# Twelve background modulation tasks move from the SSD groups to the attention heads, and a convolution's first tap from VectorE to ScalarE

## The chip, the cores and the metric

The kernel runs on one core of one Trainium2 chip. The metric is the device time of one execution in microseconds (us), the median of several runs. A core has five engines with an instruction queue each: TensorE (PE, matrix products; PEld is its weight load), VectorE (DVE), ScalarE (ACT), GpSimd (POOL) and SyncE (SP), which here issues the transfers. Each engine takes its instructions in order and waits at an instruction until its inputs are there and its output's buffer is free.

## The reference

A decoder trunk of two layers on 1024 tokens of width 1024, in float32. Layer 0 runs a Mamba-2 mixer beside a differential attention and then an MLP; layer 1 runs retention beside sliding-window attention and then an MLP. Before each sublayer the input is normalized, scaled and shifted, and after it the output is normalized and gated; scale, shift and gate are rows of a matrix product of the conditioning vector with a modulation matrix. What the change touches:

```
xbc = silu(causal_depthwise_conv(xbc, conv_w, conv_b))      # 4 taps per channel, 2048 channels
xs, Bs, Cs = split_cols(xbc, ...)                           # SSD in 4 groups of 4 heads
y = ssd_chunked(xh, dt, A, Bs, Cs)                          # 8 chunks of 128 tokens
...
q, k, v = ...                                               # differential attention: 8 heads
p = softmax(q1 k1 + bias) - lam * softmax(q2 k2 + bias)     # two maps a head, causal
out = rms_norm(p @ v)
...
shift, scale, gate = split(silu(c) @ mod_w + mod_b, 3)      # for each of 4 sublayers
```

## The kernel before, in words

Every product with a weight is made of three matmuls on float32 values that are split into a high and a low part. A weight block is loaded with one transfer of 0.5 or 1 MB into one of **two** buffers named `raw` (`raw_cols`, L163, and `load_group`, L185), its high part is cast by ACT (`wh`, L156) and its low part subtracted on POOL or DVE (`wl`, L158). Products whose results lie with features on the partitions are L454 to L456 (512 columns), those with tokens on the partitions L808 to L810 (256 columns).

The even mixer runs four SSD groups (g = 0 to 3), then the eight attention heads, then the output projection (`MixerOut`). In an SSD group the gate `zs` is made by products L808 to L810 and DVE (L843). Four convolutions (`conv`) follow, each of an ACT copy of the product into `xc` (L1006), a first tap `ch` on DVE (L1079), three more taps on DVE (L1082), a tanh on ACT (L1085) and a product on DVE (L1086); PE transposes the result (L1119). In a chunk, `xdt` on DVE (L1125) is an input of PE's L1132. In an attention head the weights of q and k (512 KB each) and, in head 0 and every second head after it, those of v for the next pair of heads (1 MB) are loaded first (`load_fm`, `v_half`). Eight query blocks follow from the widest (1024 keys) to the narrowest (128): PE makes the scores of both maps (L867, L868), DVE adds the bias and takes the maximum (L1225), ACT the exponential (L1228), DVE the reciprocals (L1233, L1234) and the difference of the maps (L1238), PE transposes it (L1245, `pat`), the copy L1247 brings it back to SBUF, PE multiplies with v (L1251, `pav`), ACT sums the squares (L1255), POOL takes the power (L135), and DVE scales the block (L1258), which SP writes out (L1260). `pat`, `pav` and `pgate` (below) share two PSUM tiles (`pt`), and the scores two larger ones.

The scheduler of the framework (it orders by a timeline of its own) sets the order of the instructions on each engine; instructions with work for later may be pulled ahead of those written before them, and PE's products for the next head stand among those of the current one, where their weights are there. Here they are called fillers.

The **background tasks** stand in a queue `bgq`: during the even mixer 12 tasks, four each for the gate of the current sublayer and the shift and the scale of the next. A task loads 1 MB of the modulation matrix into a `raw` buffer (L292) and adds it up, weighted, with two DVE operations into the only tile `macc` (L297 for the first, L299 for the others). The fourth task of each four ends with `fin`: it splits the sum into `parts` (L198 on ACT, L199 on DVE), and `parts` takes a `raw` buffer too. For the gate, PE multiplies `parts` with ones (L316, `pgate`), DVE adds the bias (L317), and SP loads `gpost` (L319), which takes the tile `macc` until DVE has used it (L320). A call of `bg()` takes `bg_n[0]` tasks from the queue; it stands in `raw_cols` and in `load_group`, so each load of weights is followed by that many tasks. `bg_n[0]` is 1 in the groups g = 2 and 3 (five calls a group), and the scheduler pulled the first of them ahead into g = 1. Ten tasks are done there, the last two in `MixerOut`.

Of the kernel before, what the change touches and what calls it, by code (L numbers as in the profile page):

```python
# [12 lines left out]
AF = mybir.ActivationFunctionType  # L13
ALU = mybir.AluOpType
# [5 lines left out]
D = 1024  # L20
# [8 lines left out]
def trunk(ctx: ExitStack, tc: tile.TileContext, x, c, rel_bias, norm_gains, mod_w, mod_b, mlp_w1, mlp_w2,  # L29
          e_w_in, e_conv_w, e_conv_b, e_dt_bias, e_A_log, e_D, e_ssd_norm, e_lambda, e_diff_norm, e_w_out,  # L30
          o_w_in, o_sinks, o_w_out, k_mat, k_onehot, k_mask, k_rope, k_ret, out, subs=(0, 1, 2, 3)):
    nc = tc.nc
# [27 lines left out]
    def turn(i):  # L60

        turns[i] = 1 - turns.get(i, 1)
        return turns[i]

    def slot(i, shape, dtype=F32, name="slot"):

        return slots.tile(shape, dtype, tag=f"s{i}", name=name)
# [73 lines left out]
    bg_n, in_mlp = [0], [False]  # L141
# [698 lines left out]
    def silu2(th, dst, src):  # L840

        nc.scalar.activation(th, src, AF.Tanh, scale=0.5)
        nc.vector.scalar_tensor_tensor(out=dst, in0=th, scalar=1.0, in1=src, op0=ALU.add, op1=ALU.mult)  # L843
# [153 lines left out]
    def even_mixer(prev, late):  # L997
# [11 lines left out]
        def silu_tmp():  # L1009
            return slot(4 + turn(4), [P, 256], F32, "th")  # L1010
# [10 lines left out]
        def z_dt(ts):  # L1021
            for t in ts:
                ps = tok_unit(z_blks, t, 272, early[t // 2][:, t % 2] if t < 4 else None)
                nc.vector.tensor_tensor(out=dt[:, t], in0=ps[:, 256:272], in1=hv[:, 0], op=ALU.add)
                silu2(silu_tmp(), zs0[t // 4][:, t % 4], ps[:, 0:256])
# [5 lines left out]
        with ExitStack() as st:  # L1031
            mp = st.enter_context(pool("ssd"))
            cw = sm[:, 6, 0:80].rearrange("p (i k) -> p i k", i=5)
            nc.vector.tensor_scalar(out=cw[:, 0:4], in0=cols[:, 1, 0:64].rearrange("p (i k) -> p i k", i=4),
                                    scalar1=0.5, scalar2=None, op0=ALU.mult)
# [9 lines left out]
            def time_steps():  # L1045
                flat = dt.rearrange("p c h -> p (c h)")
                softplus(flat)
                nc.vector.scalar_tensor_tensor(out=dA, in0=dt, scalar=-1.0,
                                               in1=hv[:, 1].unsqueeze(1).broadcast_to([P, 8, 16]),
                                               op0=ALU.mult, op1=ALU.mult)  # L1050
                nc.vector.tensor_copy(out=dAh, in_=dA)
                nc.vector.tensor_tensor(out=dAl, in0=dA, in1=dAh.bitcast(F32), op=ALU.subtract)
                for lhs, dst in ((upper, ecs), (kmat[:, 2], d2e), (ones, cdec)):
                    ps = pt.tile([P, 512], F32, tag="t", name="pcs")
                    mm(ps[:, 0:P], lhsT=lhs, rhs=dA.rearrange("p c h -> p (c h)"), start=True, stop=True)
                    nc.scalar.activation(dst.rearrange("p c h -> p (c h)"), ps[:, 0:P], AF.Exp)

            for g in range(4):
                lo_on[0] = nc.gpsimd if g else nc.vector
                zs = zs0  # L1060
                if g == 0:
                    z_dt(range(4, NT))
                    time_steps()
                    bias_rows()
                else:
                    bg_n[0] = 1 if g >= 2 else 0
                    zs = [slot(g % 2 * 6 + i, [P, 4, 256], F32, "zs") for i in range(2)]
                    proj_tok(w, g * 256, 256, lambda t, ps: silu2(silu_tmp(), zs[t // 4][:, t % 4], ps))

# [2 lines left out]
                def conv(key, ft, c0, given=None):  # L1072

                    xc, rest = given or conv_in(c0)
                    if rest:
                        rest()
                    ft_c = ft
                    h = slot(12 + turn(12), [P, D], F32, "ch")
                    nc.vector.tensor_scalar(out=h, in0=xc[:, 0:D], scalar1=cw[:, 0, ft_c:ft_c + 1],  # L1079
                                            scalar2=cw[:, 4, ft_c:ft_c + 1], op0=ALU.mult, op1=ALU.add)  # L1080
                    for i in range(1, 4):
                        nc.vector.scalar_tensor_tensor(out=h, in0=xc[:, i:i + D], scalar=cw[:, i, ft_c:ft_c + 1],  # L1082
                                                       in1=h, op0=ALU.mult, op1=ALU.add)
                    o = slot({"b": 8, "c": 9, "x0": 10, "x1": 11}[key], [P, D], F32, f"fm{key}")
                    nc.scalar.activation(o, h, AF.Tanh)  # L1085
                    nc.vector.scalar_tensor_tensor(out=o, in0=o, scalar=1.0, in1=h, op0=ALU.add, op1=ALU.mult)  # L1086
                    fm[key] = o
# [8 lines left out]
                for ci in range(NT):  # L1096
# [37 lines left out]
                    if ci:  # L1134
# [7 lines left out]
                                                   op0=ALU.mult, op1=ALU.mult)  # L1142
# [24 lines left out]
        with ExitStack() as st:  # L1167
# [6 lines left out]
            for i in range(2):  # L1174
# [5 lines left out]
                                           op0=ALU.add, op1=ALU.subtract)  # L1180
# [15 lines left out]
                             ts=range(8) if h == 0 else range(4) if h % 2 else range(4, 8))  # L1196

            lo_on[0] = nc.gpsimd
            for h in range(8):

                places = ((12, 13, 2, 3, 4, 16), (19, 18, 14, 15, 5, 17))[h % 2]
# [11 lines left out]
                for qb in reversed(range(NT)):  # L1213
# [3 lines left out]
                    for m in range(2):  # L1217
                        ps = both[:, m] if nk <= 512 else pw("psc").rearrange("p a b -> p (a b)")
                        for n0 in range(0, nk, 512):
# [16 lines left out]
                                            op0=ALU.mult, op1=ALU.mult)  # L1236
# [13 lines left out]
                    for kb in range(qb + 1):  # L1250
# [8 lines left out]
                                            op0=ALU.mult, op1=ALU.mult)  # L1259
                    nc.sync.dma_start(out=yd[2 + h // 4][:, qb, (h % 4) * P:(h % 4 + 1) * P], in_=ys)  # L1260

            lo_on[0] = nc.vector
            mo = MixerOut(0, e_w_out[0], yd, (0, 1, 2, 3), lambda g: rs if g < 2 else None,
                          lambda g, f: cols[:, 0, 120 + g * 4 + f:121 + g * 4 + f] if g < 2 else dn,
                          None)
# [328 lines left out]
```

## Time and profile before

| what | value |
|---|---|
| median of 3 runs | 3029.69 us (3027.28 to 3030.26) |
| the profiled execution's own time | 3030.93 us |
| its span from the first to the last instruction | 3029.1 us |
| instructions | 40060 |
| PE busy | 2929.4 us, 97% of the span |
| DVE, ACT, POOL busy | 66%, 43%, 16% of the span |
| mean granted TensorE clock | 0.986 |

The span is what the profiler saw; 1.8 us of the profiled execution lie around it. An engine is busy when an instruction of it is under way; instructions of one engine overlap by some hundredths of a us at their ends, so that a sum of durations is above the busy time. A granted clock of 1.00 is 2.4 GHz, 0.50 is 1.2 GHz.

### The profile page before, as it was taken

Reading aid. Unit: us, or ns where it says so; the run is one execution under the profiler, and the core shown is the slowest. Engines: PE = TensorE matmul, PEld = TensorE weight load, DVE = VectorE, ACT = ScalarE, POOL = GpSimd, SP = SyncE. Lnnn points to the kernel's source line nnn. Section 1 sums busy time; section 2 is a strip of 40 time slices with the busy share of each in tenths; the row PEclk is TensorE's granted clock in tenths of the full one; section 3 lists DMA queues with packets and bytes.
Section 4 is the critical chain, followed back from the end, with each engine's and each line's share of the span. In section 5 each row is a group of like instructions: output and inputs, shape, how many; then the busy total and the mean of one; then the engine's idle time right before and its main releaser. Section 6 shows DMA issues by size and latency. Waiting matters only on the chain.

```text
span 3029.1 us, 40060 instructions
## 1 busy us (share of the span) xinstructions
PE 2929.4 (97%) x15250; PEld 2471.4 (82%) x15250; DVE 1991.2 (66%) x3222; ACT 1309.4 (43%) x2348; POOL 474.2 (16%) x430
## 2 busy tenths in 40 slices
PE   8999999999999989999999989999999899999998
PEld 5888879888877867888888878989988678888887
DVE  5787885565586579876646845565454876666476
ACT  5232334555553264454433545432222644454333
POOL 0243443323210030000000232011101200000021
PEclk9999999999999999999999999999999999999999
DMA  6221311212142236646736542153242454476464
GB/s 215 75 89 57 120 53 46 66 41 61 46 150 71 89 127 217 221 163 235 290 125 226 191 134 63 33 168 101 84 153 77 140 188 162 153 260 231 151 223 166
DMA packets 268707, 413.59 MB, mean 137 GB/s; under 512 B 15337, under 2 KB 151138, under 8 KB 267618
## 3 DMA queue, kind: packets, MB, share of 16 engines
q1 hardware_dynamic: 268128, 410.92, 40.3%
q8 instruction: 120, 1.97, 0.3%
q14 instruction: 73, 0.60, 0.1%
q10 hardware_dynamic: 386, 0.11, 0.0%
HBM read 319.23 MB, written 91.75 MB: 136 GB/s over the span
## 4 chain that ended last, share of the span: by engine, by line
PE 81%; DVE 10%; DMA 4%; ACT 2%; issue 2%; POOL 1%; SPq 0%; POOLq 0%; DVEq 0%; ACTq 0%
PE pw L740 5%; PE pw L741 5%; PE pw L742 5%; PE pw L557 4%; PE pg L454 4%; PE pg L456 4%; PE pg L455 4%; PE pw L558 4%; PE pw L559 4%; PE pg L808 4%; PE pg L809 3%; PE pg L810 3%; PE pg L466 3%; PE pg L468 3%; PE pg L467 3%; PE pg L740 2%
## 5 line engine op out<-in xcount | busy, mean ns | idle before, releaser
L156 ACT CAST wh<-raw 128x1024 fp32r<-128x1024 f32 (+1 forms) x218 | 227.5, 1047 | 294.7 <-PE pw L558 97.7
L808 PE MATMUL pg<-wh,hh 128*128 128x256 f32 (+1 forms) x992 | 292.4, 295 | 18.5 <-DVE zs L843 10.6
L454 PE MATMUL pg<-hh,wh 128*128 128x512 f32 x736 | 292.8, 398 | 1.4 <-DVE ks L1340 0.8
L456 PE MATMUL pg<-hh,wl 128*128 128x512 f32 x736 | 291.9, 397 | 0.3 <-DVE ms L133 0.3
L455 PE MATMUL pg<-hl,wh 128*128 128x512 f32 x736 | 291.9, 397 | 0.0
L810 PE MATMUL pg<-wh,hl 128*128 128x256 f32 (+1 forms) x992 | 287.5, 290 | 0.6 <-DVE hl L439 0.6
L809 PE MATMUL pg<-wl,hh 128*128 128x256 f32 (+1 forms) x992 | 287.4, 290 | 0.0
L158 DVE TENSOR_TENSOR wl<-raw,wh 128x1024 fp32r<-128x1024 f32 (+1 forms) x162 | 199.3, 1232 | 130.3 <-ACT wh L156 127.4
L510 ACT CAST u<-uraw 128x1024 fp32r<-128x1024 f32 x112 | 117.1, 1049 | 299.8 <-PE pw L741 178.2
L511 DVE TENSOR_TENSOR u<-uraw,u 128x1024 fp32r<-128x1024 f32 x112 | 141.1, 1261 | 154.5 <-ACT u L510 153.7
L741 PE MATMUL pw<-wl,u 128*128 128x512 f32 x608 | 240.3, 395 | 0.0
L740 PE MATMUL pw<-wh,u 128*128 128x512 f32 x608 | 240.1, 396 | 0.0
L742 PE MATMUL pw<-wh,u 128*128 128x512 f32 x608 | 239.4, 394 | 0.0
L135 POOL TENSOR_TENSOR rs<-ms,expo 128x1 f32<-128x1 f32 x160 | 107.3, 671 | 682.2 <-DVE ms L133 664.2
L808 PEld LDWEIGHTS pg<-wh,hh 128*128 128x128 f32 x992 | 193.8, 195 | 21.9 <-DVE zs L843 10.3
L810 PEld LDWEIGHTS pg<-wh,hl 128*128 128x128 f32 x992 | 193.1, 195 | 2.5 <-DVE hl L439 1.3
L809 PEld LDWEIGHTS pg<-wl,hh 128*128 128x128 f32 x992 | 193.7, 195 | 1.8 <-issue 0.5
L466 PE MATMUL pg<-wh,u 128*128 128x512 f32 x448 | 181.9, 406 | 3.6 <-DVE u L940 3.1
L468 PE MATMUL pg<-wh,u 128*128 128x512 f32 x448 | 178.2, 398 | 0.0
L467 PE MATMUL pg<-wl,u 128*128 128x512 f32 x448 | 177.5, 396 | 0.0
L158 POOL TENSOR_TENSOR wl<-raw,wh 128x1024 fp32r<-128x1024 f32 x58 | 144.2, 2490 | 138.2 <-ACT wh L156 119.3
L454 PEld LDWEIGHTS pg<-hh,wh 128*128 128x128 f32 x736 | 139.1, 189 | 29.5 <-PE pg L456 1.2
(456 smaller groups left out, 7242.2 us busy)
## 6 DMA issues: line engine op xcount, KB each, us to landing
x<-in_mlp_w_dram SPq DMA_DIRECT2D x128, 512.0 KB, 6.6
uraw<-ud SPq DMA_DIRECT2D x56, 1024.0 KB, 5.5
raw<-in_mod_w_dram SPq DMA_DIRECT2D x24, 1024.0 KB, 5.0
ud<-sums SPq DMA_DIRECT2D x48, 512.0 KB, 4.2
raw<-in_mlp_w_dram SPq DMA_DIRECT2D x18, 1024.0 KB, 5.4
raw<-in_e_w_in_dram SPq DMA_DIRECT2D x32, 512.0 KB, 3.9
ud<-c SPq DMA_DIRECT2D x64, 256.0 KB, 3.1
mraw<-in_mod_w_dram SPq DMA_DIRECT2D x32, 512.0 KB, 4.9
```

The source lines that it names most:

```text
L158: lo_on[0].tensor_tensor(out=wl, in0=src, in1=wh.bitcast(F32), op=ALU.subtract)
L454: mm(ps, lhsT=wh[:, k], rhs=hh[:, k], start=(k == 0), stop=False)
L455: mm(ps, lhsT=wh[:, k], rhs=hl[:, k], start=False, stop=False)
L456: mm(ps, lhsT=wl[:, k], rhs=hh[:, k], start=False, stop=(k == 7))
L466: mm(ps, lhsT=uh[:, tl], rhs=wh[:, f % 2], start=(f == 0), stop=False)
L468: mm(ps, lhsT=ul[:, tl], rhs=wh[:, f % 2], start=False, stop=(f == 3))
L740: mm(ps[t], lhsT=uh[:, k, ts], rhs=wh[:, k], start=b, stop=False, **on)
L741: mm(ps[t], lhsT=uh[:, k, ts], rhs=wl[:, k], start=False, stop=False, **on)
L742: mm(ps[t], lhsT=ul[:, k, ts], rhs=wh[:, k], start=False, stop=e, **on)
L808: mm(ps[:, 0:n], lhsT=hh[:, k, tl], rhs=wh[:, i], start=(k == 0), stop=False)
L809: mm(ps[:, 0:n], lhsT=hh[:, k, tl], rhs=wl[:, i], start=False, stop=False)
L810: mm(ps[:, 0:n], lhsT=hl[:, k, tl], rhs=wh[:, i], start=False, stop=(k == 7))
```

## The change

`bg_n[0] = 1` is taken from the groups g = 2 and 3 and set for the loop over the eight attention heads; it is set to 0 again ahead of `MixerOut`. So the 12 tasks are called from the first 12 loads of the heads. Beside that, the first tap of each of the 16 convolutions becomes an activation with the function Identity on ACT; it reads the same tile and writes the same tile.

```diff
                 else:
-                    bg_n[0] = 1 if g >= 2 else 0
                     zs = [slot(g % 2 * 6 + i, [P, 4, 256], F32, "zs") for i in range(2)]
...
                     h = slot(12 + turn(12), [P, D], F32, "ch")
-                    nc.vector.tensor_scalar(out=h, in0=xc[:, 0:D], scalar1=cw[:, 0, ft_c:ft_c + 1],
-                                            scalar2=cw[:, 4, ft_c:ft_c + 1], op0=ALU.mult, op1=ALU.add)
+                    nc.scalar.activation(h, xc[:, 0:D], AF.Identity, scale=cw[:, 0, ft_c:ft_c + 1],
+                                         bias=cw[:, 4, ft_c:ft_c + 1])
...
             lo_on[0] = nc.gpsimd
+            bg_n[0] = 1
             for h in range(8):
...
             lo_on[0] = nc.vector
+            bg_n[0] = 0
             mo = MixerOut(0, e_w_out[0], yd, (0, 1, 2, 3), lambda g: rs if g < 2 else None,
```

Line numbers between 1080 and 1198 of the kernel before are lower by one in the changed kernel, those between 1199 and 1262 are the same.

The first place is DVE at the end of the convolutions of group g = 1, where the gate `zs` of g = 2 is made. Before:

```order
L299 SCALAR_TENSOR_TENSOR macc<-raw,cact,macc 128x1024
L1086 SCALAR_TENSOR_TENSOR fmx_1862<-fmx_1862,ch 128x1024
L299 SCALAR_TENSOR_TENSOR macc<-raw,cact,macc 128x1024
L1105 TENSOR_TENSOR rh<-kmat,dAh 128x512
L1079 TENSOR_SCALAR ch<-xc,sm 128x1024
L1114 TENSOR_TENSOR cbm<-pssd,kmat 128x128
L1082 SCALAR_TENSOR_TENSOR ch<-xc,sm,ch 128x1024
L1114 TENSOR_TENSOR cbm<-pssd,kmat 128x128
L1115 TENSOR_TENSOR dec<-dec,cbm 128x512
L1082 SCALAR_TENSOR_TENSOR ch<-xc,sm,ch 128x1024
L1115 TENSOR_TENSOR dec<-dec,cbm 128x512
L843 SCALAR_TENSOR_TENSOR zs<-th,pg 128x256
```

After:

```order
L1085 SCALAR_TENSOR_TENSOR fmc<-fmc,ch 128x1024
L1081 SCALAR_TENSOR_TENSOR ch<-xc,sm,ch 128x1024 x3
L1104 TENSOR_TENSOR rh<-kmat,dAh 128x512
L1085 SCALAR_TENSOR_TENSOR fmx_1862<-fmx_1862,ch 128x1024
L1104 TENSOR_TENSOR rh<-kmat,dAh 128x512
L1113 TENSOR_TENSOR cbm<-pssd,kmat 128x128
L1114 TENSOR_TENSOR dec<-dec,cbm 128x512
L1113 TENSOR_TENSOR cbm<-pssd,kmat 128x128
L1114 TENSOR_TENSOR dec<-dec,cbm 128x512
L1081 SCALAR_TENSOR_TENSOR ch<-xc,sm,ch 128x1024
L843 SCALAR_TENSOR_TENSOR zs<-th,pg 128x256
```

The two L299 and the L1079 ahead of the first `zs` are gone from DVE here; the other rows are the same work in nearly the same order.

The second place is SP at the entry of the attention heads. The first 256-column load of `raw` (1 MB) shown is of v's weights for heads 2 and 3, the 128-column ones are of q and k of a later head, `ye_399` is the output of the SSD and `ye_400` that of head 0. Before:

```order
L1172 DMA lam<-in_e_lambda_dram 128x256
L1144 DMA ye_399<-y 128x256 x2
L994 DMA bt_4026<-vd 128x256
L163 DMA raw<-in_e_w_in_dram 128x8x256
L994 DMA bt_4027<-vd 128x256
L163 DMA raw<-in_e_w_in_dram 128x8x128 x2
L1260 DMA ye_400<-ys 128x128 x3
L163 DMA raw<-in_e_w_in_dram 128x8x256
```

After (the task at the top is the fifth, the first of the shift):

```order
L163 DMA raw<-in_e_w_in_dram 128x8x128
L994 DMA bt_3955<-vd 128x256
L292 DMA raw<-in_mod_w_dram 128x2x1024
L1260 DMA ye_400<-ys 128x128 x5
L994 DMA bt_3954<-vd 128x256
L1260 DMA ye_400<-ys 128x128 x3
L163 DMA raw<-in_e_w_in_dram 128x8x256
L292 DMA raw<-in_mod_w_dram 128x2x1024
```

The load of v's weights for heads 2 and 3 stood ahead of all outputs of head 0 and stands now behind all eight. There it waits for PE, which must have read the gate's `parts` (made in g = 3's convolutions, where the scheduler puts the four tasks of the gate); the other `raw` buffer holds the fifth task's block, whose DVE operation needs `macc` and so stands behind `gpost`. The gate's `fin` belongs to the fourth task, which is called from head 1's first load, so that `pgate` takes its PSUM tile after those of head 0.

The third place is PE in head 0. Before, a part of its block loop, with the product for v of heads 2 and 3 (L808 to L810) between `pat` and `pav`:

```order
L808 MATMUL pg<-wh,hh_114 128x256
L809 MATMUL pg<-wl,hh_114 128x256
L810 MATMUL pg<-wh,hl_115 128x256
L454 MATMUL pg<-hh_114,wh 128x512
L455 MATMUL pg<-hl_115,wh 128x512
L456 MATMUL pg<-hh_114,wl 128x512
L454 MATMUL pg<-hh_114,wh 128x512
L455 MATMUL pg<-hl_115,wh 128x512
L1251 MATMUL pav<-v,aT 128x128 x4
L867 MATMUL psc_4681<-ks,qh 128x256
L868 MATMUL psc_4681<-ks,ql 128x256
L456 MATMUL pg<-hh_114,wl 128x512
```

After, the last rows of head 0's loop:

```order
L1245 MATMUL pat<-kmat,p 128x128 x3
L1251 MATMUL pav<-v,aT 128x128 x3
L867 MATMUL psc_4658<-ks,qh 128x128
L868 MATMUL psc_4658<-ks,ql 128x128
L1245 MATMUL pat<-kmat,p 128x128 x2
L1251 MATMUL pav<-v,aT 128x128 x2
L1245 MATMUL pat<-kmat,p 128x128
L1251 MATMUL pav<-v,aT 128x128
L316 MATMUL pgate<-parts,onesr 128x512 x4
L808 MATMUL pg<-wh,hh_114 128x256 x2
L809 MATMUL pg<-wl,hh_114 128x256
L810 MATMUL pg<-wh,hl_115 128x256
```

The products L808 to L810 for heads 2 and 3 (96 of them) and the next 48 products of 512 columns for q and k stood in head 0's loop; now they stand behind it and behind `pgate`, and in the last seven blocks of the loop scores, transposes and outputs follow each other with nothing else between them.

## Rows read from the trace of the kernel before

**Rows 1.** The page: span, and TensorE's busy time, share and instructions.
```profile
span 3029.1 us, 40060 instructions
...
PE 2929.4 (97%) x15250; PEld 2471.4 (82%) x15250; DVE 1991.2 (66%) x3222; ACT 1309.4 (43%) x2348; POOL 474.2 (16%) x430
```

**Rows 2.** Windows: us, busy us of PE, PEld, DVE, ACT, POOL (instructions), clock, DMA.
```profile
180.00:275.00 95.00, 88.70 (x516) 78.16 (x515) 81.03 (x111) 29.17 (x66) 39.05 (x34) 0.96 0.24 77
275.00:370.00 95.00, 89.32 (x523) 79.37 (x522) 79.34 (x107) 29.42 (x62) 39.49 (x32) 0.96 0.31 95
489.90:551.20 61.30, 61.30 (x380) 54.92 (x379) 36.35 (x97) 35.94 (x82) 17.50 (x14) 1.00 0.18 52
```

**Rows 3.** What PE waited for, 80 to 500 us: total, times, longest.
```profile
PE pg L808 <- DVE zs L843: 9.5, 2, 5.5
PE pxt L1119 <- DVE fmx L1086: 4.0, 2, 2.6
PE py L1132 <- DVE xdt L1125: 3.9, 2, 2.5
```

**Rows 4.** Windows in which TensorE ran at half clock.
```profile
228.10:234.90 6.80, 5.17 (x24) 5.17 (x25) 6.64 (x8) 1.06 (x1) 0.10 (x1) 0.50 0.25 104
323.70:330.50 6.80, 3.66 (x17) 3.66 (x18) 6.80 (x8) 1.05 (x1) 2.37 (x1) 0.50 0.40 136
972.20:979.00 6.80, 5.05 (x12) 3.99 (x13) 6.12 (x6) 0.48 (x1) 0.00 (x0) 0.50 0.64 195
```

**Rows 5.** DVE in time order in group g=2: start, duration, instruction.
```profile
319.01 1.27 DVE L299 SCALAR_TENSOR_TENSOR macc<-raw,cact,macc 128x1024 f32<-128x1024 f32 x1
320.20 2.85 DVE L1079 TENSOR_SCALAR ch<-xc,sm 128x1024 f32<-128x1024 f32 x1
...
326.38 0.41 DVE L843 SCALAR_TENSOR_TENSOR zs<-th,pg 128x256 f32<-128x256 f32 x1
```

**Rows 6.** Operations on the convolution's tile, durations min/median/max in ns.
```profile
L1079 DVE TENSOR_SCALAR ch<-xc,sm x16: 800/1138/2887, 88.3 to 421.8; 128x1024 f32<-128x1024 f32 x16
L1085 ACT ACTIVATE fmx<-ch x8: 1057/1060/1064, 119.0 to 428.0; 128x1024 f32<-128x1024 f32 x8
```

**Rows 7.** Operations on the accumulator of the background tasks.
```profile
L299 DVE SCALAR_TENSOR_TENSOR macc<-raw,cact,macc x42: 1259/1280/3420, 172.1 to 2139.6; 128x1024 f32<-128x1024 f32 x42
```

**Rows 8.** What PE waited for in the output projection, 960 to 990 us.
```profile
PE pg L466 <- DVE u L940: 3.1, 1, 3.1
```

**Rows 9.** DVE in time order in attention head 0.
```profile
489.99 1.23 DVE L1225 CUSTOM_DVE_ANT_0 psc<-psc,bt 128x1024 f32<-128x1024 f32 x1 [2.10 <-PE psc L868]
...
497.09 1.10 DVE L1225 CUSTOM_DVE_ANT_0 psc<-psc,bt 128x896 f32<-128x896 f32 x1 [0.83 <-PE psc L868]
...
550.82 0.41 DVE L1258 TENSOR_SCALAR ys<-pav,rs,rc 128x128 f32<-128x128 f32 x1
```

**Rows 10.** PE in time order: first and last of 15 filler matmuls.
```profile
543.77 0.40 PE L454 MATMUL pg<-hh,wh 128*128 128x512 f32 x1
...
546.98 0.39 PE L456 MATMUL pg<-hh,wl 128*128 128x512 f32 x1
```

**Rows 11.** Groups by shape, 488 to 560 us: count, busy us, mean ns.
```profile
L158 POOL TENSOR_TENSOR wl<-raw,wh 128x1024 fp32r<-128x1024 f32 x6 | 14.3, 2394 | 11.4 <-ACT wh L156 10.6 <-PE psc L868 0.8
...
L156 ACT CAST wh<-raw 128x1024 fp32r<-128x1024 f32 x5 | 5.3, 1052 | 5.6 <-PE pg L455 5.2 <-issue 0.4
...
L873 POOL MEMSET ql<- 64x1024 f32 x2 | 1.9, 949 | 0.1
...
L1228 ACT ACTIVATE p<-psc,mx 128x128 f32<-128x128 f32 x2 | 0.7, 364 | 0.3 <-DVE rc L1233 0.3
...
L1225 DVE CUSTOM_DVE_ANT_0 psc<-psc,bt 128x128 f32<-128x128 f32 x2 | 0.6, 300 | 2.6 <-PE psc L868 2.6
...
L1238 DVE SCALAR_TENSOR_TENSOR p<-p,rc 128x128 f32<-128x128 f32 x1 | 0.4, 354 | 0.0
```

**Rows 12.** DMA issues, 478 to 484 us: KB each, us to landing.
```profile
raw<-in_e_w_in_dram SPq DMA_DIRECT2D x1, 1024.0 KB, 5.2
```

## The prediction

> **What bounds the kernel now.** I read the page first: TensorE is busy 97% of the span [rows 1], so time is won only where PE stands still or runs at half clock, and lost where either is new. The windows by stage come next. In the SSD groups g=1 and g=2, PE lacks 6.3 and 5.7 us of 95, while DVE is busy 81 and 79 us and ACT only 29 in each; in attention head 0 PE is busy all 61.3 us, with DVE and ACT at 36 [rows 2]. So the moved work leaves a stage where DVE is nearly full and enters one where it has room, and the question is what order it makes there. The waits say what PE lacks in the SSD: `zs` twice (5.5 and, the rest of 9.5, 4.0 us), `fmx` (2.6 and 1.4), `xdt` [rows 3]. Each of the two `zs` waits is accompanied by 6.8 us at half clock, and so is one stretch in the output projection [rows 4]. DVE in time order shows the cause in g=2: an L299 of a background task, then an L1079 that takes 2.85 us, and only at 326.38 the `zs` for which PE waits [rows 5]. L1079 takes 0.80 us at its fastest, 1.14 in the median [rows 6].
>
> **What it gives back.** The order shows both parts at work at that place: the L299 and the L1079 ahead of `zs` are gone.
> - g=1: the `zs` wait of 4.0, the `fmx` wait of 1.4, and half of the 5.17 us for which PE worked at half clock, 2.6 [rows 3, 4]: 8.0 us.
> - g=2: 5.5, and half of 3.66, 1.8: 7.3 us [rows 3, 4].
> - g=3: nothing. Four first taps leave DVE, but the scheduler puts the gate's four tasks (eight operations of 1.28 us [rows 7]) and the split there, about as much as left. Its waits, 2.6 for `fmx` and 3.9 for `xdt` [rows 3], could go or double; I take 0, between +4 and -4.
> - Output projection: PE waited 3.1 us for `u`, which was queued on DVE behind an L299, and worked 5.05 us at half clock after it [rows 8, 4]: at most 5.6. The last two tasks leave, but a weight load of 1 MB still has to come there; I take 4.5.
>
> Sum 19.8 us, between 12 and 26. The taps' 16 activations cost nothing on ACT by this: beside them stands a tanh of the same shape at 1.06 us [rows 6], 4.2 us a group, and ACT is free for two thirds of a group.
>
> **What it takes.** The fact that decides is in the order of SP and PE. Both `raw` buffers are held through head 0: one by `parts` until `pgate`, one by the fifth task. So the load of v's weights for heads 2 and 3 cannot start before `pgate`, and `pgate` stands behind head 0's last output. The 96 products of 256 columns for that v, and 48 of 512 columns behind them, thereby leave the loop that they filled, and about as many more of 512 columns that came from head 2's early loads.
>
> *The bare loop.* Before, from the first maximum at 489.99 to the last scaled block at 550.82 [rows 9] PE was busy without a gap. Fillers come at (546.98-543.77)/14 = 0.229 us [rows 10], half of that for 256 columns. 96 of each kind are 22 and 11 us, and some 3 us are head 1's first scores, so head 0's own work on PE is about 26 us. How fast can the blocks run without fillers? From the first block's first maximum to the second block's it is 7.1 us [rows 9]: scores, two maxima, an exponential, the difference, one behind the other. The 128-wide block has two maxima of 0.30, an exponential of 0.36, a difference of 0.35 [rows 11], and about 1 us of reciprocals and hand-overs as in the wide one: 2.3 us. Eight blocks falling from 7.1 to 2.3 are 38 us, and the last block's transpose, copy, product and scaling add some 3. Laid out row by row in the new order with these durations I come to 42 us from the first maximum to `pgate`. PE idles 42-26 = 16 us. The lower bound is DVE's own work: 36.35 us [rows 2] less some 6 us for other heads, so 30, idle 4. The upper one is a loop in which PE is at half clock throughout: 52 us, loss 26.
>
> *POOL.* Two clears of 0.95 us [rows 11] stand there between the powers that the scaled blocks wait for, each behind a wait for PE: 2 us.
>
> *The clock in the loop.* In the rows of half clock, PE had stood for 4 to 5.5 us just before or within [rows 3, 4]. A loop with 16 us of gaps should be granted half clock for part of it; idle PE absorbs most of that. I take 3 us, between 0 and 10.
>
> *The wait behind it.* After `pgate`: 5.2 us of transfer [rows 12], a cast of 1.05 on ACT, a subtraction of 2.39 on POOL [rows 11]: PE stands 8.6 us. Nothing is ready in the order to cover it, since the 48 products whose weights are there stand behind. By the two `zs` waits, such a gap is followed by 6.8 us at half clock: 3.4 us more.
>
> *Heads 1 to 3.* Tasks 5 to 12 bring 16 operations of 1.28 us to a DVE that is free for 40% of the time [rows 2]; each next block is loaded when its predecessor has been added. Tasks 5 to 8 run under the 96+48 products (22 us) behind `pgate`. I take 1 us, up to 5 if the last of them delays head 1's first maximum.
>
> Sum 16+2+3+8.6+3.4+1 = 34 us. Net +14: the profiled execution's 3030.9 would become 3045; that execution lies 1.2 us above the median of the runs, so the median goes from 3029.7 to **3044 us**.
>
> **Where the skill would differ.** The row: DVE's first tap is 0.80 us when nothing disturbs it, an activation of that shape 1.06 [rows 6]. The Trainium skill, "ScalarE: Activation LUTs", section "Rules for kernel authors", says to use VectorE and not ScalarE for multiplications and additions, and budgets about 0.3 us and 0.83 ns per element for an activation, which is an estimate of 1.15 us here. It speaks against this half of the change. Priced by that rule alone, each of the 16 convolutions would be later, see the third rival. The trace does not bear it out as the deciding cost, because in the SSD it is DVE that is full.
>
> **The rivals.**
> 1. *Faster.* The loop of head 0 runs as fast as DVE allows: idle 4 to 7 us instead of 16, no half clock in it. This needs ACT and PE to keep their hand-overs hidden behind DVE. For it: DVE and ACT are both busy 36 of 61 us [rows 2], so neither is a bound at 42. Against it: the 7.1 us of the first block, in which DVE waited although PE was at full clock. Then the loss is 6+8.6+1 = 16 and with the full gain of 26 the time is 3020. It decides from a loop of about 32 us. Chance 0.18.
> 2. *No change.* The gain is 20 to 22, the loop costs 10 and the wait behind it 9 with little half clock: 3027 to 3035. Chance 0.20.
> 3. *ACT delays the convolutions.* Each tap ends 0.26 us later (1.06 for 0.80 [rows 6]) and stands in ACT's queue ahead of copies that PE waits for: 16 times 0.26 is 4 us less gain, 3048. This is the form in which the rule above would show. Against it: ACT's 29 us of 95. Chance 0.05.
> 4. *Half clock throughout.* Head 0's loop takes 52 us and the products behind it start slowly: loss 26+2+8.6+3.4+5 = 45, 3055. Chance 0.12.
>
> The forecast itself, with a loop of 38 to 46 us and 3036 to 3052, has 0.45.
>
> **The numbers.** A measurement of this kernel tells about 0.2%, 6 us, from no change. Forecast, third and fourth rival are slower (0.62), the second is within (0.20), the first is faster (0.18). The range that leaves 2 in 10 out begins inside the first rival, at a gain of 6 us, 3024, and ends at the bound of a half-clocked loop with a gain of 15, 3060; the likeliest case by itself is 3036 to 3052.
>
> **What the profile after would show.** If I am right: in g=1 and g=2 no wait for `zs` above 1 us and no half clock; L1079's place on ACT at about 1.06 us; in the window of head 0 PE busy some 60 to 65%, with waits for `aT`, `p` and ACT; `pgate` some 42 us after the first maximum; right behind it one wait of 8 to 9 us of L808 or L809 for `wh` or `wl`, and a stretch at half clock; the load of v's weights issued when `pgate` has ended. I would be wrong if that load were issued earlier, if head 0's loop took 32 us or less, or if new waits for `xc` or `ch` appeared in the SSD.

## The result, and the profile after

The changed kernel takes 3046.05 us (median of 4 runs, 3045.81 to 3051.45) against 3029.75 (3027.28 to 3030.26): ratio 1.006, 95% interval 1.0042 to 1.0077 (the ratios are not those of the medians; each experiment's is to runs of the kernel before taken beside it, with medians of 3028.89 to 3030.49). It is slower by 16.3 us, where 3044 (+14) was forecast. The profiled execution took 3051.45 us, with a span of 3049.4, so stages are compared below and not the ends.

Windows of the changed kernel (us, busy us of PE, PEld, DVE, ACT, POOL, then clock, DMA share and GB/s): g=1, g=2, head 0 from its first maximum to `pgate`, from there to the start of the products for v, and 25 us more.

```profile
180.00:275.00 95.00, 94.48 (x567) 83.92 (x566) 72.02 (x105) 37.02 (x74) 42.44 (x36) 1.00 0.15 45
275.00:370.00 95.00, 94.47 (x567) 83.95 (x566) 71.21 (x110) 35.29 (x71) 44.38 (x40) 1.00 0.20 62
473.30:514.40 41.10, 34.78 (x201) 28.47 (x199) 31.02 (x88) 24.45 (x65) 6.83 (x9) 0.97 0.11 37
514.40:526.30 11.90, 3.21 (x7) 1.48 (x7) 5.12 (x7) 2.17 (x4) 2.96 (x3) 0.50 0.59 187
526.30:551.20 24.90, 24.90 (x142) 23.02 (x143) 10.71 (x8) 4.79 (x9) 7.05 (x3) 0.88 0.40 127
```

In g=1 and g=2 PE is now busy 94.5 us of 95 at full clock [rows 2 had 88.7 and 89.3], and DVE has fallen by 8 to 9 us. Behind that: head 0 runs with PE busy 35 of 41 us (a 512-column filler's record lasts 0.39 to 0.40 us though fillers come every 0.229 us [rows 10], so the busy time of a loop with many stops is above its work), then 11.9 us with almost nothing, at half clock, and a stretch of which a quarter was at half clock.

What PE waited for in the SSD groups (total, times, longest), to be held against [rows 3]:

```profile
PE pxt L1118 <- DVE fmx L1085: 3.0, 2, 2.4
PE py L1131 <- DVE xdt L1124: 2.0, 1, 2.0
PE pg L808 <- DVE zs L843: 1.1, 2, 0.5
```

And from head 0 to head 1, where before no wait stood in the first 60 us [rows 2]:

```profile
PE pg L808 <- ACT wh L156: 6.3, 1, 6.3
PE psc L867 <- ACT p L1228: 1.8, 3, 0.9
PE pav L1251 <- ACT aT L1247: 1.7, 3, 0.7
PE pg L809 <- POOL wl L158: 1.6, 1, 1.6
...
PE pgate L316 <- DVE gg L317: 0.8, 1, 0.8
```

DVE's first maximum of head 0, and the engines in time order around `pgate`:

```profile
473.32 1.23 DVE L1225 CUSTOM_DVE_ANT_0 psc<-psc,bt 128x1024 f32<-128x1024 f32 x1 [2.04 <-PE psc L868]
```

```profile
514.37 1.22 PE L316 MATMUL pgate<-parts,onesr 128*128 128x512 f32 x2 [0.28 <-DVE ys L1258]
...
516.37 1.22 PE L316 MATMUL pgate<-parts,onesr 128*128 128x512 f32 x2 [0.79 <-DVE gg L317]
517.62 0.38 SPq L163 DMA_DIRECT2D raw<-in_e_w_in_dram  x1
...
522.77 1.99 ACT L156 CAST wh<-raw 128x1024 fp32r<-128x1024 f32 x2 [8.18 <-DMA raw<-in_e_w_in_dram]
...
523.89 2.35 POOL L158 TENSOR_TENSOR wl<-raw,wh 128x1024 fp32r<-128x1024 f32 x1 [8.49 <-ACT wh L156]
```

From the first maximum at 473.3 to `pgate` at 514.4 it is 41.1 us. SP issues v's load at 517.62, when the second pair of `pgate` is done; ACT had waited 8.18 us for it, and POOL follows. The products L808 and L809 wait 6.3 and 1.6 us.

For all kernels the stages can be told by the same rows: the last `zs` (L843) of g=0 and of g=3, the last scaled block (L1258) of head 1 and of head 5, and the last matmul of the output projection. Lengths in us between the starts of these rows, from the profiled execution of each kernel:

| kernel | g=0 to g=3 | to the end of head 1 | heads 2 to 5 | to the end of the projection | median of the runs |
|---|---|---|---|---|---|
| before | 270.4 | 264.6 | 239.2 | 241.2 | 3029.75 |
| changed | 255.8 | 290.2 | 245.8 | 239.5 | 3046.05 |
| 1: pgate in the other PSUM pair | 255.8 | 274.5 | 240.4 | 241.0 | 3029.44 |
| 2: gate called before the heads | 255.8 | 304.7 | 240.5 | 238.8 | 3056.60 |
| 3: tap alone | 260.3 | 264.1 | 239.1 | 241.1 | 3018.79 |
| 4: move alone | 262.8 | 284.9 | 245.2 | 238.8 | 3047.66 |
| 5: light additions | 255.7 | 276.6 | 246.0 | 240.4 | 3035.13 |
| 6: one buffer held | 260.4 | 265.3 | 238.2 | 240.4 | 3022.15 |
| 7: two buffers held | 261.0 | 279.7 | 242.5 | 240.3 | 3037.47 |
| 8: last two tasks in head 4 | 260.5 | 267.2 | 239.6 | 238.8 | 3022.95 |
| 9: no loads of the col tasks | 255.7 | 278.6 | 244.7 | 240.2 | 3038.25 |
| 10: gate in g=2 | 263.6 | 260.3 | 241.9 | 240.0 | 3023.46 |
| 11: tap, tasks from g=1 | 273.7 | 254.3 | 239.3 | 235.1 | 3027.03 |
| 12: no end of the gate | 255.8 | 270.4 | 239.7 | 240.3 | 3023.01 |

The change by stages: -14.6, +25.6, +6.6, -1.7, together +15.9, close to the 16.3 of the medians. Medians of the experiments come from runs that lie up to 9 us to either side of them, so differences of a few us between two experiments are read from the stages. What lies outside the stages differs among the profiled executions by some us too: the start up to the last `zs` of g=0 takes 81 to 86 us, the rest behind the projection 1927 to 1938.

The second stage can be parted at head 0's first maximum. Before, g=3 takes 136.7 us up to there and heads 0 and 1 together 127.9; in the changed kernel it is 131.9 and 158.3. So g=3 gained 4.8 us, and heads 0 and 1 lost 30.4.

### The profile page after: what moved, and what is told of

Its sections match the earlier page's. It is cut to its first block, busy times and chain, and to the rows that moved or that the text cites. A ratio compares the mean times of both kernels' runs of the same rounds, so it can differ in the third digit from the quotient of the medians.

```text
span 3049.4 us, 40036 instructions
## 1 busy us (share of the span) xinstructions
PE 2941.4 (96%) x15250; PEld 2475.2 (81%) x15250; DVE 1973.7 (65%) x3210; ACT 1327.5 (44%) x2360; POOL 468.3 (15%) x430
## 4 chain that ended last, share of the span: by engine, by line
PE 81%; DVE 8%; DMA 5%; ACT 3%; issue 1%; POOL 1%; SPq 0%; POOLq 0%; DVEq 0%; ACTq 0%
PE pw L740 5%; PE pw L741 5%; PE pw L742 5%; PE pg L454 4%; PE pg L455 4%; PE pg L456 4%; PE pw L557 4%; PE pw L559 4%; PE pw L558 4%; PE pg L808 4%; PE pg L809 4%; PE pg L810 4%; PE pg L466 3%; PE pg L468 3%; PE pg L467 3%; PE pg L740 2%
## 5 line engine op out<-in xcount | busy, mean ns | idle before, releaser
L156 ACT CAST wh<-raw 128x1024 fp32r<-128x1024 f32 (+1 forms) x218 | 227.2, 1047 | 309.0 <-PE pw L558 89.6
L808 PE MATMUL pg<-wh,hh 128*128 128x256 f32 (+1 forms) x992 | 294.8, 298 | 16.6 <-ACT wh L156 7.5
L454 PE MATMUL pg<-hh,wh 128*128 128x512 f32 x736 | 292.9, 398 | 1.7 <-DVE ql L853 0.9
L456 PE MATMUL pg<-hh,wl 128*128 128x512 f32 x736 | 291.2, 396 | 0.0
L455 PE MATMUL pg<-hl,wh 128*128 128x512 f32 x736 | 290.9, 395 | 0.0
L809 PE MATMUL pg<-wl,hh 128*128 128x256 f32 (+1 forms) x992 | 287.8, 290 | 1.6 <-POOL wl L158 1.6
L810 PE MATMUL pg<-wh,hl 128*128 128x256 f32 (+1 forms) x992 | 288.5, 291 | 0.6 <-DVE hl L439 0.6
L511 DVE TENSOR_TENSOR u<-uraw,u 128x1024 fp32r<-128x1024 f32 x112 | 141.2, 1262 | 154.5 <-ACT u L510 153.7
L741 PE MATMUL pw<-wl,u 128*128 128x512 f32 x608 | 240.3, 395 | 0.0
L808 PEld LDWEIGHTS pg<-wh,hh 128*128 128x128 f32 x992 | 195.3, 197 | 21.4 <-ACT wh L156 8.6
L809 PEld LDWEIGHTS pg<-wl,hh 128*128 128x128 f32 x992 | 195.4, 197 | 3.7 <-POOL wl L158 1.9
L810 PEld LDWEIGHTS pg<-wh,hl 128*128 128x128 f32 x992 | 194.8, 197 | 1.7 <-DVE hl L439 1.3
L454 PEld LDWEIGHTS pg<-hh,wh 128*128 128x128 f32 x736 | 138.9, 189 | 29.8 <-PE pg L456 1.2
```

Of the source, the lines that this page charges most:

```text
L454: mm(ps, lhsT=wh[:, k], rhs=hh[:, k], start=(k == 0), stop=False)
L455: mm(ps, lhsT=wh[:, k], rhs=hl[:, k], start=False, stop=False)
L456: mm(ps, lhsT=wl[:, k], rhs=hh[:, k], start=False, stop=(k == 7))
L741: mm(ps[t], lhsT=uh[:, k, ts], rhs=wl[:, k], start=False, stop=False, **on)
L808: mm(ps[:, 0:n], lhsT=hh[:, k, tl], rhs=wh[:, i], start=(k == 0), stop=False)
L809: mm(ps[:, 0:n], lhsT=hh[:, k, tl], rhs=wl[:, i], start=False, stop=False)
```

## The experiments

The theory was that of the prediction: the two `raw` buffers are held until `pgate`, which stands behind head 0, and this empties head 0's loop and makes v's load late. The rival: 16 more additions on DVE make the heads slower, wherever `pgate` is.

**1. `pgate` takes its PSUM tile from another pair.** The tasks stay in the heads.

```diff
-                ps = pt.tile([P, 512], F32, tag="t", name="pgate")
+                ps = pg.tile([P, 512], F32, tag="g", name="pgate")
```

> The changed kernel, with one edit: pgate takes its PSUM tile from the pair of the products (pg) and not from the pair of the transposes and outputs (pt), so that it no longer stands behind head 0's tiles; the tasks stay in the heads. Theory (the loss comes from the two raw buffers that are held until pgate, which empties head 0's loop and makes the load of v late): PE's order has 112 products of 256 columns and 110 of 512 in head 0's loop again, the wait of 8 us behind pgate and the stretch at half clock there are gone, the loop's fillers hide about 15 us; 3046 less 23 to 30 = 3016 to 3023, below the kernel before. Rival (the heads lose because 16 more operations of 1.28 us stand on DVE there, wherever pgate is): 3043 to 3049.

Measured: 3029.44 us, ratio to before 1.0002 (0.9993 to 1.001). One line gives back 16.6 us: head 0's loop has its fillers again (271 products from its first maximum to its last scaled block, against 240 before and 48 in the changed kernel), and no wait for a weight stands behind `pgate`. The edit is in a helper that the gates of the other sublayers use too; behind the projection this kernel takes 1928.7 us, like the others, so the gain is not from there. But it is 6 us above the range of the theory, far below that of the rival, and the stage to the end of head 1 is still 9.9 us longer than before (heads 0 and 1 take 144.5 us, 16.6 more than before and 13.8 less than in the changed kernel). So the held buffers are the larger part of the loss and not all of it.

**2. The gate's tasks called ahead of the heads.**

```diff
             bg_n[0] = 1
+            for _ in range(4):
+                bgq.popleft()()
             for h in range(8):
```

> The changed kernel, but the four tasks of the gate are called just ahead of the loop over the heads, and tasks 5 to 12 from the loads in the heads as in the changed kernel. Theory (held raw buffers): pgate stands ahead of head 0's tiles in program order, head 0's loop has its 96 and 115 fillers, 3016 to 3024. Rival (DVE work in the heads): tasks 5 to 12 come even earlier in the heads, 3043 to 3049.

Measured: 3056.6 us, ratio 1.0092 (1.0075 to 1.0109). Both expectations failed. Head 0 keeps its fillers as the theory has it, but the four loads now stand ahead of head 0's own weights. The window 370 to 470 us, the end of g=3 and the entry of the heads:

```profile
370.00:470.00 100.00, 77.16 (x325) 60.72 (x325) 74.11 (x118) 31.00 (x69) 38.07 (x38) 0.80 0.21 67
```

PE is busy 77 us of 100 and the clock is at 0.80. The loss has moved one stage ahead, to the entry of head 0. Yet the trace shows the theory's wait again: no load of `raw` is issued between 370.61, when the fifth task's block is, and 449.14, when the second pair of `pgate` is done.

```profile
447.89 1.22 PE L316 MATMUL pgate<-parts,onesr 128*128 128x512 f32 x2 [0.78 <-DVE gg L317]
...
449.14 0.38 SPq L163 DMA_DIRECT2D raw<-in_e_w_in_dram  x1
```

So both buffers are held until `pgate` here too, now ahead of head 0's own weights. To call the gate earlier only moved the hold.

**3 and 4. The two halves of the change, one at a time.** Third run: the kernel before with `nc.scalar.activation(h, xc[:, 0:D], AF.Identity, ...)` as the first tap and no other edit. Fourth run: the changed kernel with `nc.vector.tensor_scalar(...)` as the first tap.

> The kernel before with the first tap as an activation on ACT and nothing else; the tasks stay in the SSD groups. PE's order in the heads is that of before. Theory (DVE full in g=1 and g=2, waits for zs are caused by L299 and L1079 together): part of the 15 us there goes, since L299 still stands ahead of zs: gain 3 to 8, 3022 to 3027, with zs waits left of 2 to 6 us. Rival (the tap was all of it, the tasks do no harm there): gain 13 to 16, 3014 to 3017. Second rival (the activation of 1.24 us makes every convolution later and PE waits for it): 3031 to 3036.

> The changed kernel with the first tap back on VectorE; only the tasks are moved. PE's order in the heads is that of the changed kernel, with a bare loop in head 0. Theory: the loss of some 32 us behind the first maximum is all there, and of the gain of 16.7 us ahead of it 8 to 13 are left, because the zs waits needed both operations: 3049 to 3055. Rival (the tap does nothing): 3045 to 3047.

Measured: 3018.79 us for the tap alone, ratio 0.9969 (0.9958 to 0.9981), and 3047.66 for the move alone, 1.0064 (1.0052 to 1.0077). In the stage from g=0 to g=3 the tap gains 10.1 us and the move 7.6; both together gain 14.6, less than the 17.7 of the sum. What PE waited for there, tap alone and then move alone:

```profile
PE pg L808 <- DVE zs L843: 5.4, 3, 3.9
PE py L1132 <- DVE xdt L1125: 3.6, 2, 2.2
PE pxt L1119 <- DVE fmx L1086: 0.7, 1, 0.7
```

```profile
PE pg L808 <- DVE zs L843: 4.8, 2, 2.4
PE pxt L1118 <- DVE fmx L1085: 3.0, 2, 1.7
```

Each half leaves part of the wait for `zs` (9.5 before, 1.1 with both), so either operation can be the one that is too much for DVE. In the changed kernel the tap's worth is not clear of the noise (3047.66 to 3046.05, with runs that overlap): of its 7.0 us in g=1 to g=3, 5.3 are gone again by the end of head 1. The tap alone gained more than the 3 to 8 us expected and less than the 13 to 16 of its rival, and the move alone came out between the two ranges, 1.3 us below that of the theory. The tap costs nothing later: all other stages are within 0.5 us of before. The kernel with the tap alone is the fastest of the study, faster than the kernel before and the changed one.

**6 and 7. The suspected cost, without the move.** To the kernel with the tap alone, one or two tiles of the raw ring are added that PE reads where the changed kernel has `pgate`:

```diff
-                wq, wk = load_fm(w, 3088 + h * P, 1)[0], load_fm(w, 4112 + h * P, 1)[0]
+                wq = load_fm(w, 3088 + h * P, 1)[0]
+                if h == 1:
+                    for _ in range(2):
+                        held = wp.tile([P, 2, D], F32R, tag="raw", name="held", bufs=2)
+                        nc.vector.tensor_copy(out=held[:, 0, 0:P], in_=ident)
+                        ps = pt.tile([P, 512], F32, tag="t", name="phold")
+                        mm(ps[:, 0:P], lhsT=onesr, rhs=held[:, 0, 0:P], start=True, stop=True)
+                        hm = stat.tile([P, 1], F32, tag="hold", name="hold", bufs=1)
+                        nc.vector.tensor_copy(out=hm, in_=ps[:, 0:1])
+                wk = load_fm(w, 4112 + h * P, 1)[0]
```

> The kernel with the tap alone (3018.8, tasks in the SSD groups), and one extra tile of the raw ring that DVE fills with 128 columns and that PE reads, in a PSUM tile of the pair of transposes, at the place where the changed kernel has pgate, after head 0. It adds one small copy, one matmul and one read. Theory (only when both raw buffers are held does v's load have to wait): the other buffer passes the loads on, head 0's loop keeps 96 and 99 fillers, 3017 to 3024. Rival (one held buffer is enough): 3034 to 3044.

> As the run before, with two such tiles, so that both raw buffers are held until PE has read them after head 0; no task is moved. Theory: the changed kernel's loss without any task in the heads: bare loop (no fillers in head 0), load of v after it, wait of 8 us and half clock: 3018.8 plus 18 to 26 = 3037 to 3045. Rival (the bare loop costs little, the loss is that of the tasks' work in the heads): 3019 to 3026.

Measured: 3022.15 us with one, 3037.47 with two. With one buffer held, every stage stays within 1.2 us of the tap alone. With two, the stage to the end of head 1 grows by 15.6 us, and the kernel by 18.7 to the tap alone. PE in heads 0 and 1 of that kernel waits for a weight's cast and split, as in the changed kernel:

```profile
PE pg L454 <- ACT wh L156: 4.8, 1, 4.8
...
PE pg L456 <- POOL wl L158: 1.2, 1, 1.2
```

With no task in the heads this makes 19 us of loss (15.6 and 3.4 in the stages to the end of head 1 and of heads 2 to 5), where the changed kernel lost 25.6 and 6.6, and it shows that it takes both buffers. Heads 0 and 1 take 143.2 us, 15.3 more than with the tap alone: nearly the 13.8 that the first experiment took away.

**5 and 9. What is left: additions or transfers?** Both start from the first experiment. The fifth shortens the additions of the shift and scale tasks:

```diff
+                    n = P if s == 1 and third < 2 and k else D
...
-                        nc.vector.scalar_tensor_tensor(out=acc, in0=raw[:, i], scalar=cact[:, k:k + 1], in1=acc,
-                                                       op0=ALU.mult, op1=ALU.add)
+                        nc.vector.scalar_tensor_tensor(out=acc[:, 0:n], in0=raw[:, i, 0:n], scalar=cact[:, k:k + 1],
+                                                       in1=acc[:, 0:n], op0=ALU.mult, op1=ALU.add)
```

The ninth leaves out their loads and adds up `hT[0][0][:, i * 2:i * 2 + 2]`, which is in SBUF, in place of `raw[:, i]`.

> The kernel of the first experiment (pgate in the other PSUM pair), in which the additions of the shift and scale tasks of the next sublayer (14 of 16, in the heads) take only 128 of 1024 columns; transfers, buffers and order of waits stay. It leaves out that part of the modulation sum. In the first experiment the stretch from the gate of g=3 to the end of head 5 was still 11 us longer than before, with PE waits for p and aT where an L299 stood on DVE. Theory (the additions on DVE delay the chain of maxima and differences): these 11 us go nearly all, 3029 less 8 to 12 = 3017 to 3021. Rival (the 1 MB transfers, which take every second place in the two raw buffers, make the heads' weights late): 3026 to 3032.

> The kernel of the first experiment (pgate in the other PSUM pair, 3029.4) without the transfers of the eight shift and scale tasks of the next sublayer: their 16 additions stay on DVE at full width, but read a tile that is in SBUF anyway and take no raw buffer. It leaves out what these transfers bring, so that this shift and scale are other numbers. The light additions of the fifth run gave nothing back (3035), so the remaining 11 us should lie with the transfers. Theory (tasks and weights take turns in two raw buffers, so that the next head's weights come late and its fillers are missing where PE waits for p): 3029 less 8 to 14 = 3015 to 3021. Rival (the additions after all, the light ones having been undone by another order): 3026 to 3032.

Measured: 3035.13 and 3038.25 us, both above the 3029.44 of the first experiment and above every range given; neither theory nor rival foresaw that. The scheduler made another order in each, so that they do not isolate what they were meant to. In the ninth all 16 additions, with no transfer to wait for, were crowded into head 0 (10 of them in the first experiment), which takes 93.3 us from its first maximum to its last block against 77.9 in the first experiment. From the last scaled block of head 0 to that of head 1, though, it is 66.6 us in the first experiment, 64.9 in the fifth, 54.2 in the ninth and 59.7 before: without the loads head 1 is no longer slower, with light additions it is. But the ninth has 311 products in head 0 and 183 in head 1, the first experiment 271 and 220, so a shorter head 1 is in part work that was done earlier. Heads 0 and 1 together take 144.5, 143.3 and 147.5 us in the first, fifth and ninth (127.9 before). So lighter additions, at nearly the same places, gave back 1.2 us of 16.6 there, and taking the loads away gave nothing back: these two runs do not show which of the two costs the time.

The trace of the first experiment shows one way in which the shared buffers cost time. SP, DVE and ACT in time order there, near the end of head 1:

```profile
576.61 0.38 SPq L292 DMA_DIRECT2D raw<-in_mod_w_dram  x1
...
584.18 0.37 SPq L163 DMA_DIRECT2D raw<-in_e_w_in_dram  x1
```

```profile
581.55 2.60 DVE L299 SCALAR_TENSOR_TENSOR macc<-raw,cact,macc 128x1024 f32<-128x1024 f32 x2 [0.50 <-DMA raw<-in_mod_w_dram]
```

```profile
585.36 0.47 ACT L1228 ACTIVATE p<-psc,mx 128x256 f32<-128x256 f32 x1
...
589.48 1.99 ACT L156 CAST wh<-raw 128x1024 fp32r<-128x1024 f32 x2 [3.57 <-DMA raw<-in_e_w_in_dram]
...
592.21 0.46 ACT L1247 COPY aT<-pat 128x384 f32<-128x384 f32 x1
```

A task's block is loaded at 576.61; DVE's two additions end at 584.15 and free the buffer; at 584.18 SP issues the load of v's weights into it. ACT, in its order, stands 3.57 us at the cast L156 for that load, and behind the cast stands `aT`, for which PE waits:

```profile
PE pav L1251 <- ACT aT L1247: 3.2, 1, 3.2
```

That is 3.2 of the 5.6 us that PE lacks between 580 and 612.

**10 and 12. The gate's end.** The tenth run is the changed kernel with `bg_n[0] = 1 if g == 2 else 0` put back into the SSD, so that the gate's tasks and one of the shift's are called there. The twelfth is the first experiment without `parts`, `pgate` and the addition of the gate's bias.

> The changed kernel, but the gate's four tasks (and one of the shift) are called in g=2 as before, and only the other seven from the heads; pgate is then done in the SSD, and head 0 keeps its fillers (117 and 99). Theory: the 21 us of the held buffers are gone, the SSD keeps most of its gain of 10 to 15, seven tasks share the raw buffers in the heads at about 1 us each: 3018 to 3026. Rival (tasks in the heads cost as much without the gate): 3038 to 3047.

> The kernel of the first experiment (pgate in the other PSUM pair, 3029.4) without the end of the gate's sum: parts, pgate and the addition to the bias are left out for this sublayer (its gate is the bias alone), all transfers and additions of the twelve tasks stay. In the first experiment heads 0 and 1 still lost 13 us to the kernel before, and with the gate's tasks in g=2 (tenth run) only 3. Theory (what is left of the loss lies in the gate's end at head 0's entry: parts in a raw buffer, pgate, two L317 and L320 ahead of the fifth task on DVE): 3029 less 7 to 11 = 3018 to 3022, heads 0 and 1 within 5 us of before. Rival (it lies with the tasks of shift and scale in heads 0 and 1): 3026 to 3031, head 1 still 6 us and more longer.

Measured: 3023.46 us, ratio to before 0.9978 (0.9969 to 0.9988), and 3023.01 us, 0.9978 (0.9968 to 0.9988). With the gate in g=2 the theory held: the stage to the end of head 1 is not longer than before (260.3 against 264.6), and heads 2 to 5 are 2.7 us longer. The seven tasks called from the heads are not free, though: the scheduler put their additions into g=3 and head 0, and heads 0 and 1 together take 132.6 us, 4.7 more than before. Without the gate's end, the stage to the end of head 1 is 4.1 us shorter than in the first experiment, short of the 7 to 11 expected, and the two places of the loss come apart. Windows of the first experiment and, below, of the twelfth: the entry of head 0, and the end of head 1:

```profile
455.00:490.00 35.00, 31.72 (x152) 25.59 (x152) 25.92 (x42) 16.99 (x32) 13.66 (x7) 1.00 0.42 132
...
580.00:612.00 32.00, 26.37 (x156) 23.33 (x155) 25.20 (x60) 17.62 (x44) 9.25 (x9) 0.89 0.28 92
```

```profile
455.00:490.00 35.00, 35.00 (x190) 30.09 (x189) 26.06 (x45) 19.62 (x36) 14.07 (x8) 1.00 0.51 165
...
580.00:612.00 32.00, 26.36 (x150) 23.47 (x150) 24.79 (x60) 16.02 (x41) 9.25 (x9) 0.84 0.25 79
```

At the entry PE goes from 31.7 us to all 35. At the end of head 1 nothing changes: 26.4 of 32 us and part of it at half clock, in both. Each side of that expectation had one half of it.

**8 and 11. Versions that might beat the tap alone.** The eighth calls the last two tasks from head 4 on; the eleventh sets `bg_n[0] = 1` from g=1 on.

> The kernel with the tap alone, and the last two tasks (of the scale), which it has in the output projection, called from head 4's loads. Theory: the output projection's wait of 3 us for u behind an L299 and the half clock after it go, worth 2 to 4; two tasks in a head cost what they cost in the first experiment, about 1 us a task: 3016 to 3020, same as the tap alone or a little below. Rival (the full 5.6 of my prediction is there and the heads hide the tasks): 3012 to 3015.

> The kernel with the tap alone, and the tasks called from g=1 on, so that all twelve lie in the SSD groups and none in the output projection. Theory: the output projection gains 2 to 4 us (no wait for u behind an L299), the SSD takes two more tasks on a DVE that is busy 78 to 81 of 95 us and loses 1 to 4: 3015 to 3022, no different from the tap alone (3018.8). Rival (DVE in g=1 is over its limit with tasks there): 3023 to 3030.

Measured: 3022.95 us, ratio 0.9978 (0.9969 to 0.9987), and 3027.03, 0.999 (0.9981 to 0.9999). Neither is better than the tap alone, and the eighth lies above both its ranges. Against the tap alone the output projection gains 2.3 and 6.0 us. The eighth gives 3.1 back ahead of the end of head 1, where the scheduler has pulled the first of the two tasks; the eleventh loses 13.4 us from g=0 to g=3 and gains 9.8 in the next stage. Its time lies in the range of the rival, that DVE has no room for more tasks there.

## Why the prediction was right

- **The gain in g=1 and g=2** was summed to 8.0 + 7.3 = 15.3 us from the waits and the half-clock stretches; the stage from g=0 to g=3 is 14.6 us shorter. Experiments 3 and 4 show that both halves of the change work at the same waits.
- **g=3** was put at nothing, between +4 and -4. Up to head 0's first maximum it is 4.8 us shorter; the move alone has 130.6 us there and the tap alone 136.2, against 136.7 before, so this is the move's. The gate's end at head 0's entry was left out of the forecast: in the order of experiment 1 it costs 4 us.
- **The bare loop** was laid out at 42 us and took 41.1, but it was not bare, and the step from there to 16 us of idle PE was wrong. The scaled block at 550.82 [rows 9] is the seventh of eight; the last starts at 558.16, behind 144 products of 512 columns (L454 to L456, 48 each) and not 96. Of these, 48 stayed in the changed kernel's loop. The 192 products that left it are 33 us of work at 0.229 us for 512 columns [rows 10] and half that for 256, and from the first maximum to the last scaled block head 0 became 25.3 us shorter (68.2 to 42.9). So the loop without them cost about 8 us, or 12 with head 1's first scores, some 4 us, that left it too: an estimate from these rows. The records show 6.3 us of idle PE, and PE busy 85% of the loop where 60 to 65% was to be the sign. The rows are the last scaled block of before, its products L454 from 489.99 to 558.16 (L455 and L456 have the same count), and those of the changed kernel from 473.3 to 514.4:

```profile
558.16 0.41 DVE L1258 TENSOR_SCALAR ys<-pav,rs,rc 128x128 f32<-128x128 f32 x1
```

```profile
L454 PE MATMUL pg<-hh,wh 128*128 128x512 f32 x48 | 19.0, 395 | 0.0
```

```profile
L454 PE MATMUL pg<-hh,wh 128*128 128x512 f32 x16 | 6.3, 392 | 0.0
```

- **The wait behind `pgate`** was 8.6 us and is 6.3 + 1.6 by the records, in the order that was given: transfer, cast, split. The half clock behind it: all of 11.9 us, and 12% short of full in 24.9 us, which is 6 us at half; predicted 6.8. In the loop the clock was 0.97, so the 3 us for it there were too much. (Of the three rows on which that was priced, one stood behind a wait of 3.1 us [rows 8] and not of 4 to 5.5.)
- **Both together** were 33 us in heads 0 and 1 (loop 16, POOL 2, clock 3 + 3.4, wait 8.6), and these heads lost 30.4. But only part of that belongs to the held buffers: without the hold (experiment 1) heads 0 and 1 are 13.8 us shorter, and the hold without the tasks (experiment 7) makes them 15.3 longer. In the kernel's time the two experiments put it at 17 to 19 us. So the mechanism was right and its price about twice too high; no run tells the 2 us of POOL apart.
- **Heads 1 to 3** were mis-sized: 1 us, up to 5. With the hold gone, heads 0 and 1 are still 16.6 us longer than before: that is what the tasks and the gate's end cost in that order. I had looked at DVE's free time and not at the two buffers, which tasks and weights use by turns; in experiment 1 that shows as a late weight, a cast that stands, and `aT` behind it, in one place. The 6.6 us in heads 2 to 5 are mostly not the tasks' own work: with the same tasks and no hold it is 1.2, with the hold and no task there 3.4 over the tap alone.
- **The output projection** was mis-sized: 4.5 us; the stage is 1.7 shorter.
- **The third rival** did not show: the tap takes 1.24 us on ACT (row below), more than the tanh's 1.06 [rows 6] on which I had priced it, and still PE waits for neither `xc` nor `ch` in the list of waits of the SSD above.

```profile
L1078 ACT ACTIVATE ch<-xc,sm x16: 1229/1242/1255, 90.2 to 402.3; 128x1024 f32<-128x1024 f32 x16
```

By the Trainium skill, "ScalarE: Activation LUTs", section "Rules for kernel authors", multiplications and additions belong on VectorE. Here the tap is slower on ACT than DVE's undisturbed 0.80 us [rows 6], and yet the kernel with this edit alone is 10 us faster, so the measurement decides against the rule in this place: with DVE busy 81 us of 95 and ACT 29 [rows 2], what counts is whose queue it stands in.

That the net came out at +16 with +14 forecast is in part luck. By stages the errors are of both signs: 4.8 us of gain in g=3 and 2.6 us less loss in heads 0 and 1 than forecast (33 for 30.4) against 6.6 us in heads 2 to 5 and 2.8 in the projection. And within heads 0 and 1 the hold was priced at 33 us and is worth 14 to 15, while the tasks and the gate's end, put at 1, cost about as much again.

What stays open: why the order of the fifth kernel, with shorter additions, is slower in heads 2 to 5 by 5.6 us than that of the first experiment; how the loss in heads 0 and 1 of the changed kernel splits between the missing fillers and the wait; and whether the tasks cost there by their transfers, their additions or the order that the scheduler makes with them. A kernel with a third raw buffer or one for the tasks alone, which could have told this, was not run.

## What to carry to other kernels

Work that is moved to where an engine has room takes its buffers along: before moving it, ask in which ring its tiles lie, which instruction frees them, and what that instruction stands behind in program order. Two tiles that wait for one matmul behind a loop stopped a ring of two for the whole loop, and one line, another PSUM pair for that matmul, gave 17 us back. When an edit has two halves, run each alone: here the smaller half was the gain.

## What the runs showed of the hardware that I had not expected

The activation Identity with a scale and a bias for each partition takes 1.24 us on 128x1024 (1229 to 1255 ns in 16 instances), the tanh of the same shape without them 1.06 us [rows 6].
